# ReLU and row mean of a 67 MB array on one core: a second block of one row to a partition, and 126 rows a partition in place of 127

## The chip, the cores and the metric

One core of a Trainium2 chip. The metric is the device time of one execution in microseconds (us).

## The reference

```python
x = np.random.randn(32, 512, 1024).astype(np.float32)   # 16,384 rows of 4 KiB
np.mean(np.maximum(x, 0), axis=-1)                       # 16,384 results
```

## The kernel before

The first 128 rows are loaded one to a partition (a "block"). They come first and give ScalarE (ACT) early work; its table load of 1.28 us falls there. The other 16,256 rows are cut into 128 runs of J = 127, one run for each partition, so that rows of neighbouring partitions lie 127 x 4 KiB = 508 KiB apart in HBM. They come as seven full tiles of 16 rows a partition through three buffers, then pieces of 7, 4, 2 and 1 rows, then the last row in three pieces of columns. SyncE issues every transfer; the trace books each in packets, here one for each partition. ACT takes the even rows, VectorE (DVE) the odd ones; each writes one sum a row.

```python
xfirst, xmain = xf[:P, :], xf[P:, :]
outfirst, outmain = out.flatten()[:P], out.flatten()[P:]
J = J - 1                                     # 127
xr = xmain.rearrange("(p j) d -> p j d", p=P, j=J)
...
row_pieces = [7, 4, 2, 1]
col_pieces = [512, 256, 256]
...
for t in range(full):                         # 7 tiles, BUFS = 3, NB = 16
    buf_free(t)                               # waits for the tile 3 back to be consumed
    if t == 0:
        load(-1, row0[:, :], xfirst)          # the block: 128 packets of 4 KiB
    load(t, bufs[t % BUFS][:, :, :], xr[:, t * NB:(t + 1) * NB, :])   # 128 packets of 64 KiB
    if t == BUFS:
        nc.sync.wait_ge(first, 2)
        nc.sync.dma_start(                    # the block's results: 4 rows of 32 numbers
            out=outfirst.rearrange("(q i) -> q i", i=32), in_=turned0[0:P:32, :],
        ).then_inc(stored, 16)
... # pieces of rows, then of columns
nc.sync.dma_start(out=outr, in_=res[:, :]).then_inc(stored, 16)       # 128 rows of 508 B
...
nc.sync.wait_ge(stored, 32).then_inc(stored, -32)                     # the program's last wait
```

The block's 128 means lie one to a partition; DVE transposes them so that they leave as 4 rows of 128 B.

Of the kernel before, what the change touches and what calls it, by code (L numbers as in the profile page):

```python
# [9 lines left out]
ACT = mybir.ActivationFunctionType  # L10
# [35 lines left out]
def kernel(  # L46
# [10 lines left out]
    nc = tc.nc  # L57
    P = nc.NUM_PARTITIONS
    xf = x.flatten_outer_dims()
    R, D = xf.shape  # L60
    assert R % P == 0
    J = R // P
    inv = 1.0 / D

    xfirst, xmain = xf[:P, :], xf[P:, :]
    outfirst, outmain = out.flatten()[:P], out.flatten()[P:]
    J = J - 1
    xr = xmain.rearrange("(p j) d -> p j d", p=P, j=J)
    outr = outmain.rearrange("(p j) -> p j", p=P, j=J)

    NB = 16
    BUFS = 3
    full = J // NB

    row_pieces = [7, 4, 2, 1]
    assert full * NB + sum(row_pieces) + 1 == J
    col_pieces = [512, 256, 256]
    assert sum(col_pieces) == D

    def sbuf(name, *shape):  # L80
        return ctx.enter_context(nc.sbuf_tensor(name, list(shape), F32))

    bufs = [sbuf(f"rows{b}", P, NB, D) for b in range(BUFS)]
    sums, res, part = sbuf("sums", P, J), sbuf("res", P, J), sbuf("part", P, 2)


    last = sbuf("last", P, D + 2)
    scale = sbuf("scale", P, D // 4 + 2)

    row0, mean0, turned0 = sbuf("row0", P, D), sbuf("mean0", P, 32), sbuf("turned0", P, 32)  # L90


    loaded = [nc.alloc_semaphore(f"loaded{i}") for i in range(full + len(row_pieces) + len(col_pieces) + 1)]
    act, dve, pool = (nc.alloc_semaphore(n) for n in ("act", "dve", "pool"))
    first = nc.alloc_semaphore("first")
    stored = nc.alloc_semaphore("stored")
# [11 lines left out]
    def load(i, dst, src):  # L108
        nc.sync.dma_start(out=dst, in_=src).then_inc(loaded[i], 16)

    def buf_free(t):

        if t >= BUFS:
            nc.sync.wait_ge(act, t - BUFS + 1)
            nc.sync.wait_ge(dve, t - BUFS + 1)

    for t in range(full):
        buf_free(t)
        if t == 0:
            load(-1, row0[:, :], xfirst)  # L120
        load(t, bufs[t % BUFS][:, :, :], xr[:, t * NB:(t + 1) * NB, :])
        if t == BUFS:

            nc.sync.wait_ge(first, 2)
            nc.sync.dma_start(
                out=outfirst.rearrange("(q i) -> q i", i=32), in_=turned0[0:P:32, :],
            ).then_inc(stored, 16)
    j0 = full * NB
    buf_free(full)
    xt = bufs[full % BUFS]  # L130
    lo, i = 0, full
    for n in row_pieces:
        load(i, xt[:, lo:lo + n, :], xr[:, j0 + lo:j0 + lo + n, :])
        lo, i = lo + n, i + 1
    c = 0
    for w in col_pieces:
        load(i, last[:, c:c + w], xr[:, J - 1, c:c + w])
        c, i = c + w, i + 1
# [5 lines left out]
    def rows(i, xt, lo, n, j0):  # L144
        nc.scalar.wait_ge(loaded[i], 16)
        nc.vector.wait_ge(loaded[i], 16)
        for k in range(lo, lo + n):
            j = j0 + k
            done = (dve_row if j % 2 else act_row)(nc, xt[:, k, :], sums[:, j:j + 1])
            if k >= lo + n - 2:  # L150
                done.then_inc(dve if j % 2 else act, 1)

    def finish(after, lo, hi):

        nc.gpsimd.wait_ge(act, after)
        nc.gpsimd.wait_ge(dve, after)
        nc.gpsimd.tensor_scalar(  # L157
            out=res[:, lo:hi], in0=sums[:, lo:hi], scalar1=inv, scalar2=0.0, op0=ALU.mult, op1=ALU.add,
        )

    nc.scalar.wait_ge(pool, 1)
    nc.vector.wait_ge(pool, 1)
    nc.scalar.wait_ge(loaded[-1], 16)
    nc.scalar.activation(  # L164
        out=row0[:, :], in_=row0[:, :], func=ACT.Relu, scale=inv, accum_out=mean0[:, 0:1],
    ).then_inc(first, 1)
    nc.vector.wait_ge(first, 1)
    nc.vector.transpose(turned0[:, :], mean0[:, :]).then_inc(first, 1)  # L168
    for t in range(full):
        rows(t, bufs[t % BUFS], 0, NB, t * NB)  # L170
    finish(full, 0, j0)
    lo, i = 0, full
    for n in row_pieces[:-1]:
        rows(i, xt, lo, n, j0)
        lo, i = lo + n, i + 1
# [12 lines left out]
        out=res[:, J - 2:J - 1], in0=part[:, 0:1], scalar1=part[:, 1:2], scalar2=inv, op0=ALU.add, op1=ALU.mult,  # L188
# [9 lines left out]
        out=last[:, 768:], in0=last[:, 768:], scalar=0.0, in1=scale[:, :], op0=ALU.max, op1=ALU.mult,  # L198
        accum_out=res[:, J - 1:J],
# [7 lines left out]
    used = [s.num for s in (*loaded, act, dve, pool, first)]  # L207
    assert used == list(range(used[0], used[0] + len(used)))
    nc.sync.sem_clear(range(used[0], used[-1] + 1))
    nc.sync.wait_ge(stored, 32).then_inc(stored, -32)  # L210

    for e, hint in zip(hinted, hints):
        e.br_lt(flag, 1, on_true="rows_begin", on_false="rows_end").branch_hint(hint)
# [34 lines left out]
```

## Time and profile before

| what | value | from |
|---|---|---|
| device time, median of 3 | 161.46 us (161.40 to 161.55) | the runs |
| span of the profiled execution | 160.2 us | page |
| transfer engines busy | 97.7% | page, queue line |
| DVE / ACT busy | 46% / 44% | page |
| one full tile of 8.39 MB | 19.34 to 19.50 us | its landing times in the timeline |
| last packet of the loads ended | 157.38 us | records of single packets |
| last byte of the final store / its completion | 159.76 / 160.21 us | the same |

The page and the timeline lines that carry the reading are in the prediction.

```profile
SPq L115 <- DVE rows L20: 104.6, 5, 29.5
SPq L204 <- DVE last L197: 45.6, 1, 45.6
SPq L210 <- SPq L210: 1.2, 1, 1.2
```

The first line is SyncE waiting for buffers to come free, far ahead of need; the second is the wait for the last arithmetic; the third is the wait for the final store to be confirmed, and nothing runs beside it. It is 1.2 us of pure path.

### The profile page before, as it was taken

Reading aid. Unit: us, or ns where it says so; the run is one execution under the profiler, and the core shown is the slowest. Engines: PE = TensorE matmul, PEld = TensorE weight load, DVE = VectorE, ACT = ScalarE, POOL = GpSimd, SP = SyncE. Lnnn points to the kernel's source line nnn. Section 1 sums busy time; section 2 is a strip of 40 time slices with the busy share of each in tenths; the row PEclk is TensorE's granted clock in tenths of the full one; section 3 lists DMA queues with packets and bytes.
Section 4 is the critical chain, followed back from the end, with each engine's and each line's share of the span. In section 5 each row is a group of like instructions: output and inputs, shape, how many; then the busy total and the mean of one; then the engine's idle time right before and its main releaser. Section 6 shows DMA issues by size and latency. Waiting matters only on the chain. (4 is left out here: it accounts for less than half of the span.)

```text
span 160.2 us, 347 instructions
## 1 busy us (share of the span) xinstructions
DVE 73.3 (46%) x131; ACT 70.4 (44%) x133; POOL 1.3 (1%) x9
## 2 busy tenths in 40 slices
DVE  0000029900498006960079500993009920299984
ACT  1400029800496006950079300991009900299983
POOL 1000000000000000000000000000000000000001
DMA  9969969979989899699699699699699797998992
GB/s 393 507 278 523 507 278 523 442 344 523 409 376 523 360 425 524 294 491 523 262 524 523 262 523 524 262 523 523 262 524 458 327 523 327 425 451 367 419 412 102
DMA packets 2312, 67.18 MB, mean 419 GB/s; under 512 B 392, under 2 KB 648, under 8 KB 1032
## 3 DMA queue, kind: packets, MB, share of 16 engines
q1 hardware_dynamic: 2312, 67.18, 97.7%
HBM read 67.11 MB, written 0.07 MB: 419 GB/s over the span
## 5 line engine op out<-in xcount | busy, mean ns | idle before, releaser
L20 DVE TENSOR_SCALAR_CACHE_REDUCE rows<-rows 128x1024 f32<-128x1024 f32 (+1 forms) x63 | 72.1, 1208 | 78.9 <-DMA rows<-in_x_dram 78.7
L15 ACT ACTIVATE rows<-rows 128x1024 f32<-128x1024 f32 x64 | 66.2, 1035 | 84.1 <-DMA rows<-in_x_dram 83.9
L15 ACT ACTIVATION_READ_ACCUMULATOR rows<-rows 128x1 f32 x64 | 11.9, 186 | 0.0
L20 DVE DVE_READ_ACCUMULATOR rows<-rows 128x1 f32 x63 | 5.2, 82 | 0.0
L168 DVE STREAM_TRANSPOSE turned<-mean 128x32 f32<-128x32 f32 x1 | 0.2, 213 | 5.9 <-ACT row L164 5.9
L164 ACT ACT_TABLE_LOAD x1 | 1.3, 1283 | 3.3 <-DMA row<-in_x_dram 3.3
L157 POOL TENSOR_SCALAR res<-sums 128x112 f32<-128x112 f32 (+1 forms) x2 | 0.5, 250 | 154.0 <-DVE rows L20 154.0
L164 ACT ACTIVATE row<-row 128x1024 f32<-128x1024 f32 x1 | 1.1, 1056 | 0.0
L15 ACT ACTIVATE last<-last 128x512 f32<-128x512 f32 x1 | 0.6, 630 | 0.0
L20 DVE TENSOR_SCALAR_CACHE_REDUCE last<-last 128x256 f32<-128x256 f32 x1 | 0.4, 420 | 0.3 <-DMA last<-in_x_dram 0.3
L197 DVE SCALAR_TENSOR_TENSOR last<-last,scale 128x258 f32<-128x258 f32 x1 | 0.4, 428 | 0.1
L142 POOL MEMSET scale<- 128x258 f32 x1 | 0.3, 314 | 0.0
L187 POOL TENSOR_SCALAR res<-part 128x1 f32<-128x1 f32 x1 | 0.3, 267 | 0.6 <-DVE rows L20 0.6
L164 ACT ACTIVATION_READ_ACCUMULATOR row<-row 128x1 f32 x1 | 0.2, 186 | 0.0
L15 ACT ACTIVATION_READ_ACCUMULATOR last<-last 128x1 f32 x1 | 0.2, 186 | 0.0
L141 POOL MEMSET mean<- 128x32 f32 x1 | 0.1, 126 | 1.5 <-POOLq L55 1.5
L232 POOL MEMSET const-uint8-127<- 128x1 uint8 x1 | 0.1, 103 | 0.0
L232 POOL MEMSET const-bfloat16-1.0<- 128x1 bf16 x1 | 0.1, 102 | 0.0
L232 POOL MEMSET const-float32-0.0<- 128x1 f32 x1 | 0.1, 99 | 0.2 <-issue 0.2
L232 POOL MEMSET const-float32-1.0<- 128x1 f32 x1 | 0.1, 99 | 0.0
L20 DVE DVE_READ_ACCUMULATOR last<-last 128x1 f32 x1 | 0.1, 83 | 0.0
L197 DVE DVE_READ_ACCUMULATOR last<-last,scale 128x1 f32 x1 | 0.1, 82 | 0.0
## 6 DMA issues: line engine op xcount, KB each, us to landing
rows<-in_x_dram SPq DMA_DIRECT2D x1, 3584.0 KB, 38.1
rows<-in_x_dram SPq DMA_DIRECT2D x1, 2048.0 KB, 42.6
rows<-in_x_dram SPq DMA_DIRECT2D x1, 1024.0 KB, 44.7
row<-in_x_dram SPq DMA_DIRECT2D x1, 512.0 KB, 3.3
rows<-in_x_dram SPq DMA_DIRECT2D x1, 512.0 KB, 45.4
last<-in_x_dram SPq DMA_DIRECT2D x1, 256.0 KB, 45.6
last<-in_x_dram SPq DMA_DIRECT2D x2, 128.0 KB, 45.4
rows<-in_x_dram SPq DMA_DIRECT2D x7, 48.8
```

Of the source, the lines that this page charges most:

```text
L15: return nc.scalar.activation(out=src, in_=src, func=ACT.Relu, accum_out=acc)
L20: return nc.vector.tensor_scalar(out=src, in0=src, scalar1=0.0, scalar2=init, op0=ALU.max, op1=ALU.add, accum_out=acc,)
L141: nc.gpsimd.memset(mean0[:, :], 0.0)
L142: nc.gpsimd.memset(scale[:, :], inv).then_inc(pool, 1)
L157: nc.gpsimd.tensor_scalar(out=res[:, lo:hi], in0=sums[:, lo:hi], scalar1=inv, scalar2=0.0, op0=ALU.mult, op1=ALU.add,)
L164: nc.scalar.activation(out=row0[:, :], in_=row0[:, :], func=ACT.Relu, scale=inv, accum_out=mean0[:, 0:1],).then_inc(first, 1)
L168: nc.vector.transpose(turned0[:, :], mean0[:, :]).then_inc(first, 1)
L187: nc.gpsimd.tensor_scalar(out=res[:, J - 2:J - 1], in0=part[:, 0:1], scalar1=part[:, 1:2], scalar2=inv, op0=ALU.add, op1=ALU.mult,).then_i ...
L197: nc.vector.scalar_tensor_tensor(out=last[:, 768:], in0=last[:, 768:], scalar=0.0, in1=scale[:, :], op0=ALU.max, op1=ALU.mult, accum_out=r ...
L232: nc = _bacc.Bacc("TRN2", target_bir_lowering=False, num_devices=1)
```

## The change

A second block of 128 rows is taken out of the main part. J falls from 127 to 126, the distance between partitions from 508 to 504 KiB, the first short piece from 7 to 6 rows. The second block is loaded ahead of tile 2, behind the second full tile. Both blocks' means leave later, in two stores. The total of bytes is the same. What might be hoped for is one row less to compute a partition behind the last full tile, and a different pitch in HBM.

```diff
-    xfirst, xmain = xf[:P, :], xf[P:, :]
-    outfirst, outmain = out.flatten()[:P], out.flatten()[P:]
-    J = J - 1
+    xfirst, xmain = xf[:2 * P, :].rearrange("(c p) d -> p c d", c=2), xf[2 * P:, :]
+    outfirst, outmain = out.flatten()[:2 * P], out.flatten()[2 * P:]
+    J = J - 2
...
-    row_pieces = [7, 4, 2, 1]
+    row_pieces = [6, 4, 2, 1]
...
-        if t == 0:
-            load(-1, row0[:, :], xfirst)
+        if t in (0, 2):
+            c = t // 2
+            load(c - 2, row0[:, c, :], xfirst[:, c, :])
         load(t, bufs[t % BUFS][:, :, :], xr[:, t * NB:(t + 1) * NB, :])
-        if t == BUFS:
+        if t == BUFS + 2:
 
             nc.sync.wait_ge(first, 2)
-            nc.sync.dma_start(
-                out=outfirst.rearrange("(q i) -> q i", i=32), in_=turned0[0:P:32, :],
-            ).then_inc(stored, 16)
+            for c in range(2):
+                nc.sync.dma_start(
+                    out=outfirst[c * P:(c + 1) * P].rearrange("(q i) -> q i", i=32), in_=turned0[c:P:32, :],
+                ).then_inc(stored, 16)
... (ACT takes block c ahead of tile 0 and tile 2; DVE transposes behind the second)
-    nc.sync.wait_ge(stored, 32).then_inc(stored, -32)
+    nc.sync.wait_ge(stored, 48).then_inc(stored, -48)
```

More of the change, by code (lines that the diff above doesn't have):

```diff
@@ L88 @@
     scale = sbuf("scale", P, D // 4 + 2)
-    row0, mean0, turned0 = sbuf("row0", P, D), sbuf("mean0", P, 32), sbuf("turned0", P, 32)
-    loaded = [nc.alloc_semaphore(f"loaded{i}") for i in range(full + len(row_pieces) + len(col_pieces) + 1)]
+    row0, mean0, turned0 = sbuf("row0", P, 2, D), sbuf("mean0", P, 32), sbuf("turned0", P, 32)
+    loaded = [nc.alloc_semaphore(f"loaded{i}") for i in range(full + len(row_pieces) + len(col_pieces) + 2)]
     act, dve, pool = (nc.alloc_semaphore(n) for n in ("act", "dve", "pool"))
@@ L162 @@
     nc.vector.wait_ge(pool, 1)
-    nc.scalar.wait_ge(loaded[-1], 16)
-    nc.scalar.activation(
-        out=row0[:, :], in_=row0[:, :], func=ACT.Relu, scale=inv, accum_out=mean0[:, 0:1],
-    ).then_inc(first, 1)
-    nc.vector.wait_ge(first, 1)
-    nc.vector.transpose(turned0[:, :], mean0[:, :]).then_inc(first, 1)
-    for t in range(full):
+    for t in range(full):
+        if t in (0, 2):
+            c = t // 2
+            nc.scalar.wait_ge(loaded[c - 2], 16)
+            done = nc.scalar.activation(
+                out=row0[:, c, :], in_=row0[:, c, :], func=ACT.Relu, scale=inv, accum_out=mean0[:, c:c + 1],
+            )
+            if c == 1:
+                done.then_inc(first, 1)
+                nc.vector.wait_ge(first, 1)
+                nc.vector.transpose(turned0[:, :], mean0[:, :]).then_inc(first, 1)
         rows(t, bufs[t % BUFS], 0, NB, t * NB)
```

## The prediction

> **What bounds the kernel now.** I read the page first: the strip of 40 slices, the queue line, and the two costliest groups.
>
> ```profile
> DMA  9969969979989899699699699699699797998992
> q1 hardware_dynamic: 2312, 67.18, 97.7%
> HBM read 67.11 MB, written 0.07 MB: 419 GB/s over the span
> ...
> L20 DVE TENSOR_SCALAR_CACHE_REDUCE rows<-rows 128x1024 f32<-128x1024 f32 (+1 forms) x63 | 72.1, 1208 | 78.9 <-DMA rows<-in_x_dram 78.7
> L15 ACT ACTIVATE rows<-rows 128x1024 f32<-128x1024 f32 x64 | 66.2, 1035 | 84.1 <-DMA rows<-in_x_dram 83.9
> ```
>
> The packets of the one queue fill 97.7% of the 16 transfer engines' span. VectorE (DVE) and ScalarE (ACT) are each idle longer (78.9 and 84.1 us) than they are busy, nearly all of it waiting for the input. The dips to 6 in the strip are no gaps: a packet is booked where it starts and lasts 2.4 us of a 4 us slice. So next I asked for busy time by stage, taking as edges the moments at which the full tiles landed (when DVE and ACT start on them together).
>
> ```profile
> core 0: us, DVE busy (x) ACT busy (x) POOL busy (x), PEclk, DMA share, GB/s
> 42.32:61.69 19.37, 9.21 (x16) 8.42 (x16) 0.00 (x0) 1.00 1.00 433
> 61.69:81.05 19.36, 9.21 (x16) 8.43 (x17) 0.00 (x0) 1.00 1.00 433
> 81.05:100.40 19.35, 9.21 (x16) 8.42 (x16) 0.00 (x0) 1.00 1.00 434
> ```
>
> Every 8.39 MB tile takes 19.35 to 19.37 us with the transfer share at 1.00, and leaves DVE 10.1 us of slack. The kernel is a stream of 67.11 MB at 433 GB/s with a short start and a short tail. The tail I read from the timeline (start us, us, instruction, the idle time before it):
>
> ```profile
> 139.30 1.22 DVE L20 TENSOR_SCALAR_CACHE_REDUCE rows<-rows 128x1024 f32<-128x1024 f32 x1 [10.29 <-DMA rows<-in_x_dram]
> ...
> 152.71 1.22 DVE L20 TENSOR_SCALAR_CACHE_REDUCE rows<-rows 128x1024 f32<-128x1024 f32 x1 [0.79 <-DMA rows<-in_x_dram]
> ...
> 155.20 1.22 DVE L20 TENSOR_SCALAR_CACHE_REDUCE rows<-rows 128x1024 f32<-128x1024 f32 x1
> ...
> 156.49 0.75 DVE L20 TENSOR_SCALAR_CACHE_REDUCE rows<-rows 128x576 f32<-128x576 f32 x1
> ...
> 157.54 0.42 DVE L20 TENSOR_SCALAR_CACHE_REDUCE last<-last 128x256 f32<-128x256 f32 x1 [0.29 <-DMA last<-in_x_dram]
> ...
> 158.06 0.43 DVE L197 SCALAR_TENSOR_TENSOR last<-last,scale 128x258 f32<-128x258 f32 x1
> ...
> 158.57 0.35 SPq L205 DMA_DIRECT2D out_dram<-res  x1
> ```
>
> The last full tile is at hand at 139.30, the piece of four rows at 152.71, and the second column piece of the last row at 157.54. Each is still waited for, so the stream sets the tail too. From that last landing on, two short DVE instructions and the store follow in series.
>
> **What the Trainium skill says.** (1) "DMA: Bandwidth & Descriptors", section "Where 436 GB/s comes from", puts the ceiling of the 16 ports at 435.2 GB/s; the trace's 433 is 99.5% of it. (2) The same page, "Latency and other measured facts", in its entry on the HBM row pitch at large powers of two, has copies slow down at pitches of 512 KiB and beyond (207 GB/s at 512 KiB, 103 at 4 MiB) and recover with 4 KiB of padding. The pitch between partitions here is 127 rows of 4 KiB, 508 KiB, and becomes 504 KiB; the 433 GB/s agree that 508 is clean, and no trace yet shows 504. (3) The same page, "Why small descriptors are slow", states a fixed overhead for each packet; the trace has it, below. (4) The same page, "Why a DMA increments its semaphore by 16 and not by 1", derives how many engines share a transfer from the slowest dimension of its patterns: a store of 4 partitions uses 4 engines. The trace has just four packets of 128 B for it.
>
> **The change part by part.** The records of single packets in the trace give the median time of one packet by size, where all engines are busy: 65,536 B 2,420 ns; 28,672 B 1,062; 16,384 B 611; 4,096 B 159; 1,024 B 46. These lie on a line: (2,420 - 1,062)/36,864 = 0.0368 ns a byte, and 159 - 4,096 x 0.0368 = about 8.3 ns fixed. That is all I need to price the loads:
>
> - *Removed:* one of seven rows from the first short piece. Its 128 packets shrink from 28,672 to 24,576 B, 1,062 to about 913 ns. At 8 packets for each engine: 8 x 149 = 1.19 us less.
> - *Added:* a second block load of 128 packets of 4,096 B: 8 x 159 = 1.27 us for each engine, and one more completion write (9 ns). Bytes are unchanged; the sum is 8 x 8.3 ns + 9 ns = **about +0.08 us, and all of it on the path**, as the stream has no gap.
> - *Moved:* the block goes between tiles 1 and 2, so that tiles 2 to 6 land 1.27 us later and the pieces behind them only 0.08 us later. Three buffers are loaded ahead, and the issues of the later loads ran 27 us or more before their packets, so no transfer starts late.
> - *Compute:* one ACT row of 1.06 us + 0.19 us (its accumulator read) comes behind tile 1, into an idle stretch of 10.9 us; DVE's transpose (0.21 us) moves there and waits for it, inside its own 10.1 us. Neither reaches tile 2, expected near 61.69 + 1.27 = 62.96. The table load of 1.28 us still hides behind the first block. In the first short piece DVE keeps 3 rows and ACT goes from 4 to 3.
> - *Store:* two stores of 512 B in place of one, later. Each takes about 0.63 us of the issuing queue with two tiles of packets still ahead, and four packets of 13 ns. Nothing. The final store has 504 B a row instead of 508 (27 ns a packet): nothing.
> - *Tail:* tile 6 lands later (139.30 + 1.27 + a little = 140.6), while what follows it does not. DVE needs 1.14 us a row: 8 rows until 149.7, 3 rows of the short piece until 153.1. The piece of four landed at 152.8, so here DVE is 0.3 us late where it had been 0.79 us early. Two rows: 155.4, against 155.3 of the piece of two; one row: 156.55, against 156.57 for the next landing. The lateness is gone by then, and another 0.29 us lie before the column piece. ACT, at 1.04 us a row, finishes the short piece near 152.2 and is never late. So the tail moves by the stream's 0.08 us alone.
>
> Sum: 161.46 + 0.08 = 161.54; with a few hundredths for a crowded tail, **161.55 us**.
>
> **The rivals.** *The pitch matters.* Multiples of 8 KiB instead of 4 KiB could make the streams of the 16 engines meet in the same part of HBM more often. For it speaks point (2), where powers of two are costly; against it that 504 KiB is 63 x 8 KiB, far from a large power of two, and that the present stream is held by the ports and not by HBM, which leaves HBM some reserve. If each 64 KiB packet took 3% longer, 2,420 to 2,493 ns, the 56 of them for each engine would add 4.1 us: 165.6 us. Half of that would still be called the same.
> *The pitch helps.* It can't by much: from 433.3 to 435.2 GB/s is 0.4% of 154.9 us, 0.7 us: 160.8 us at the least.
> *DVE becomes the end of the tail.* The margin above is 0.02 us at the piece of one row and 0.29 us behind it. If the later tile costs DVE 0.5 us more than I worked out, the end moves by perhaps 0.2 us: 161.75 us. Speaks for it that DVE has no idle time left between 140.6 and 157.4; against it that its rows took 1.14 us without a change all through the trace.
> *The block's load is slow in mid-stream.* The first packets of the first block took up to 656 ns (the trace's records), but those started on idle engines; the 4,096 B packets of the one-row piece, in the stream, took 159. If all eight took 300 ns, it would add 1.1 us: 162.7 us. I give it little.
>
> **Range and chances.** The three runs of before spread 0.15 us. Around 161.55 I allow 0.35 us below for another draw of the stream's rate and 0.55 us above for the tail and a slightly worse pitch: 161.2 to 162.1. Faster by 2% would be below 158.2, under the floor of the ports: 0.01. Slower by 2% is above 164.7; only the pitch could do that: 0.05. Within 2%: 0.94.
>
> **What would show it.** Right: tile 2 waited for until about 63.0 instead of 61.69, the intervals of the later tiles again 19.35 to 19.4 us, 24,576 B packets near 913 ns, 4,096 B ones at 159; in the tail no wait of DVE before the pieces of four and two rows, but still one before the column piece, at about 157.6. Wrong: 64 KiB packets clearly off 2,420 ns, in either direction (the pitch); DVE's last wait gone (the tail); a longer stretch between tiles 1 and 2 than 19.37 + 1.3 us (the block); a transfer share under 1.00 in any stage between full tiles (a late issue).

## The result, and the profile after

The changed kernel took 161.72 us (median of 6 runs, 161.50 to 162.07) against 161.43 us of the kernel before in the same rounds (161.26 to 161.78). The ratio is 1.0016, with a 95% interval of 1.0000 to 1.0032: the same. A ratio is the mean time of one kernel's fast runs over that of the other's of the same rounds, so it is not quite the ratio of the medians.

The page of the changed kernel, the same lines:

```profile
DMA  9969969979996996996996996996998998899991
q1 hardware_dynamic: 2464, 67.18, 97.5%
HBM read 67.11 MB, written 0.07 MB: 419 GB/s over the span
...
L20 DVE TENSOR_SCALAR_CACHE_REDUCE rows<-rows 128x1024 f32<-128x1024 f32 (+1 forms) x63 | 71.9, 1208 | 84.7 <-DMA rows<-in_x_dram 84.7
```

There are 2,464 packets instead of 2,312, the same bytes, and the queue is as full as before. DVE's idle time grew only because its early wait for the block's transpose is now a wait for tile 0. By stage, from landing to landing of the full tiles (us, busy times, clock, transfer share, GB/s):

```profile
42.44:63.06 20.62, 9.42 (x17) 9.46 (x18) 0.00 (x0) 1.00 1.08 465
63.06:82.42 19.36, 9.21 (x17) 8.43 (x17) 0.00 (x0) 1.00 1.00 433
82.42:101.76 19.34, 9.21 (x16) 8.42 (x17) 0.00 (x0) 1.00 1.00 434
101.76:121.11 19.35, 9.20 (x16) 8.42 (x16) 0.00 (x0) 1.00 1.00 434
```

The first row holds tile 2 and the block: 20.62 us where the same stage had 19.37, so the block took 1.25 us of the stream. (Its share over 1 is the booking of packets where they start.) The stages behind it are the old 19.35 us. The tail, from the timeline:

```profile
140.46 1.22 DVE L20 TENSOR_SCALAR_CACHE_REDUCE rows<-rows 128x1024 f32<-128x1024 f32 x1 [10.14 <-DMA rows<-in_x_dram]
...
153.00 1.21 DVE L20 TENSOR_SCALAR_CACHE_REDUCE rows<-rows 128x1024 f32<-128x1024 f32 x1
...
155.28 1.22 DVE L20 TENSOR_SCALAR_CACHE_REDUCE rows<-rows 128x1024 f32<-128x1024 f32 x1
...
156.45 0.75 DVE L20 TENSOR_SCALAR_CACHE_REDUCE rows<-rows 128x576 f32<-128x576 f32 x1
...
157.48 0.42 DVE L20 TENSOR_SCALAR_CACHE_REDUCE last<-last 128x256 f32<-128x256 f32 x1 [0.27 <-DMA last<-in_x_dram]
...
158.00 0.43 DVE L203 SCALAR_TENSOR_TENSOR last<-last,scale 128x258 f32<-128x258 f32 x1
...
158.51 0.35 SPq L211 DMA_DIRECT2D out_dram<-res  x1
```

The last tile came 1.16 us later (140.46 against 139.30), DVE no longer waited before the piece of four rows (153.00), and the lateness was gone before the column piece, for which it again waited 0.27 us. The final store was issued at 158.51, even 0.06 us earlier than before. Yet the span is 160.5 us, not 160.2. The rest is in SyncE's own waits (waited for: us in total, times, longest):

```profile
SPq L210 <- DVE last L203: 40.8, 1, 40.8
SPq L216 <- SPq L216: 1.5, 1, 1.5
```

The last line is the wait for the final store, 1.5 us against 1.2. In the packet records the last byte of that store was moved at 159.70 us and its last completion arrived at 160.43, 0.73 us later; before, these were 159.76 and 160.21, 0.44 us. So of the 0.22 us between the two spans, -0.06 lie ahead of the store's last byte and +0.28 behind it (0.726 less 0.444). I had priced the stores at nothing.

The -0.06 does not mean that the packets cost nothing. In the profile of the kernel before, the last two stages were slower than the 19.35 us of the others:

```profile
100.40:119.80 19.40, 9.20 (x16) 8.42 (x16) 0.00 (x0) 1.00 1.00 432
119.80:139.30 19.50, 9.21 (x16) 8.42 (x17) 0.00 (x0) 1.00 0.93 400
```

Counted in packets: the time by which 65,536 B packets exceeded 2,418 ns, added up and divided by the 16 engines, is 0.67 us there and 0.42 us in the changed kernel's profile, 0.25 us less. With the 0.08 us of added packets the loads should then have ended about 0.17 us earlier, and they did (157.21 against 157.38 us). A single pair of profiles can't show the packet price without this correction.

### The profile page after: what moved, and what is told of

Same layout as the page of the kernel before. It is cut to its first block, busy times and chain, and to the rows that moved or that the text cites. A ratio compares the mean times of both kernels' runs of the same rounds, so it can differ in the third digit from the quotient of the medians.

```text
span 160.5 us, 349 instructions
## 1 busy us (share of the span) xinstructions
DVE 73.1 (46%) x131; ACT 70.3 (44%) x133; POOL 1.3 (1%) x9
## 2 busy tenths in 40 slices
DMA packets 2464, 67.18 MB, mean 419 GB/s; under 512 B 416, under 2 KB 672, under 8 KB 1184
## 3 DMA queue, kind: packets, MB, share of 16 engines
q1 hardware_dynamic: 2464, 67.18, 97.5%
## 5 line engine op out<-in xcount | busy, mean ns | idle before, releaser
L15 ACT ACTIVATE rows<-rows 128x1024 f32<-128x1024 f32 (+1 forms) x63 | 65.2, 1035 | 84.2 <-DMA rows<-in_x_dram 84.0
L169 ACT ACTIVATE row<-row 128x1024 f32<-128x1024 f32 x2 | 2.1, 1048 | 0.0
```

The source lines that it names most:

```text
L15: return nc.scalar.activation(out=src, in_=src, func=ACT.Relu, accum_out=acc)
L169: done = nc.scalar.activation(out=row0[:, c, :], in_=row0[:, c, :], func=ACT.Relu, scale=inv, accum_out=mean0[:, c:c + 1],)
```

## The experiments

Two theories were on the table for a difference this small. **A**: only the packets cost (+0.08 us), the rest is spread. **B**: the final store's confirmation is really slower. The doubts that the prediction had left, pitch and block, were tested beside them. All times are medians; "before" is the kernel before in the same rounds.

### again: the changed kernel unaltered

> The changed kernel, unaltered, in five rounds. Theory A (only the packets cost): the ratio to the kernel before is 1.0005 (+0.08 us), and the +0.26 us of the first rounds was run-to-run spread. Theory B (the final store is slower with rows of 504 B than of 508 B: in the two profiles the last loads were done within 0.17 us of each other, and the wait behind the store lasted 1.5 us against 1.2): the ratio stays near 1.0016 (+0.26 us), and the wait behind the store is again 1.4 to 1.5 us. An interval that holds both leaves it open.

Measured: 161.62 us against 161.57 (ratio 1.0004, interval 0.9988 to 1.0021). The interval holds 0.08 us and 0.26 us alike. The wait behind the store was again long:

```profile
SPq L216 <- SPq L216: 1.4, 1, 1.4
```

Pooling this with the first rounds, the changed kernel's 12 runs average 161.74 us and the 17 of the kernel before 161.54: 0.20 us, an eighth of a per cent. By the spread of these runs that is uncertain by about 0.17 us either way (two standard errors), so 0.08 us is not excluded.

### pitch508 and pitch512: the distance between partitions alone

```diff
-    xr = xmain.rearrange("(p j) d -> p j d", p=P, j=J)
+    xr = xf[P:, :].rearrange("(p j) d -> p j d", p=P, j=J + 1)[:, :J, :]    # pitch508
+    xr = xf.rearrange("(p j) d -> p j d", p=P, j=J + 2)[:, :J, :]           # pitch512
```

> The changed kernel with one thing undone: the rows of the full tiles and pieces are read 127 rows apart from partition to partition (508 KiB) instead of 126 (504 KiB), so the result is wrong on purpose, and packets, sizes and order are the same. If the pitch of 504 KiB costs nothing (my prediction), this takes the changed kernel's time within 0.15 us, and the 65,536 B packets stay at 2,418 to 2,420 ns. If 504 KiB costs the 0.2 us that the first rounds showed beyond the packets, this is 0.2 us faster.

> The same with partitions 128 rows apart (512 KiB), wrong on purpose. The Trainium skill's entry on row pitches gives 207 GB/s at 512 KiB against 214 at full rate for copies. If that holds for one-way loads too, the 65,536 B packets take 3% longer (2,490 ns) and the time is near 166 us. If the load stream is held by the ports and HBM has reserve, nothing changes: 161.7 us, and then a pitch of 504 KiB can't matter either.

Measured, both with the wrong result they were meant to have: 161.71 us at 508 KiB (ratio 1.0006, 0.9990 to 1.0023) and 161.81 us at 512 KiB (1.0013, 0.9992 to 1.0034), before 161.57. The changed kernel in the same rounds had 161.62. The 65,536 B packets had a median of 2,418 ns in all three. The stages between full tiles of the kernel with 512 KiB:

```profile
63.32:82.67 19.35, 9.21 (x17) 8.43 (x17) 0.00 (x0) 1.00 1.00 434
82.67:102.04 19.37, 9.21 (x17) 8.43 (x17) 0.00 (x0) 1.00 1.01 433
102.04:121.49 19.45, 9.20 (x16) 8.42 (x16) 0.00 (x0) 1.00 1.00 431
```

The stream runs at 431 to 434 GB/s even at the distance that I thought the risky one. A 3% loss, 4 us, is excluded; a few tenths of a microsecond are not, by the interval. The pitch is no lever for this kernel.

### store508, store508_again: the changed kernel with the old stores

```diff
-            for c in range(2):
+            for c in range(1):
...
-    outr = outmain.rearrange("(p j) -> p j", p=P, j=J)
+    outr = outmain.rearrange("(p j) -> p j", p=P, j=J + 1)     # res has a filler column
...
-    nc.sync.wait_ge(stored, 48).then_inc(stored, -48)
+    nc.sync.wait_ge(stored, 32).then_inc(stored, -32)
```

> The changed kernel with the stores of the kernel before: one store of 512 B and a final store of 128 rows of 508 B (the last column is filler, the result is wrong on purpose), loads and arithmetic as in the changed kernel. Theory A: the changed kernel's time, within 0.1 us. Theory B: 0.2 us faster than the changed kernel, and the wait behind the final store back at 1.2 us from 1.5.

> The same program as in the run with the old stores, which came out 0.29% slower than the kernel before where theory B wanted it level and theory A 0.05% slower. If that was an effect of the program, it repeats: about 1.003. If it was chance, this lands between 0.999 and 1.0015.

Measured: 161.98 us (ratio to before 1.0029, 1.0010 to 1.0049), and in another set of rounds 161.99 us (1.0026, 1.0013 to 1.0038). Neither theory had that: putting the old stores back did not make it faster but, if anything, slower than the changed kernel (by the means 0.28 us in the same rounds, 162.03 against 161.74), and the distance to the kernel before repeats. Why it is slower than the changed kernel stays open. The wait behind the store:

```profile
SPq L217 <- SPq L217: 1.5, 1, 1.5
```

It stayed long with rows of 508 B. So theory B as I had put it, that rows of 504 B alone are the cause, falls.

### control: the kernel before against itself

> The kernel before against itself, to learn how far two identical programs come apart. If the interval that the rounds give is honest, the ratio lies within 0.1% of 1. If a difference of 0.2 to 0.3 us shows here too, then neither the +0.26 us of the first rounds of the change nor the +0.4 us of the run with the old stores can be read as an effect. Its profile is a second look at the wait behind the final store: 1.2 us again if that is a property of the kernel, 1.2 to 1.7 if it is spread.

Measured: 161.59 us against 161.47, ratio 1.0000, interval 0.9987 to 1.0013. Identical programs agree to about 0.13%, 0.2 us. This is the grain of every figure here. The wait behind its final store:

```profile
SPq L210 <- SPq L210: 1.3, 1, 1.3
```

### before_store504: the kernel before with the new stores alone

```diff
-    outr = outmain.rearrange("(p j) -> p j", p=P, j=J)
+    outr = outmain.rearrange("(p j) -> p j", p=P, j=J - 1)
... (two early stores of 512 B as in the change, the final one of res[:, :J - 1])
```

> The kernel before with the stores of the changed one alone: two stores of 512 B and a final store of 504 B a row (one result column and some rows go amiss, wrong on purpose); loads and arithmetic as before. Theory A: 1.000, within 0.1%. Theory B (these stores cost 0.2 us): 1.0015 and a wait behind the final store of 1.4 us or more.

Measured: 161.79 us against 161.47, ratio 1.0022, interval 1.0008 to 1.0036, with the old loads untouched. The wait:

```profile
SPq L211 <- SPq L211: 1.5, 1, 1.5
```

The interval leaves out theory A's 1.000, though not quite the tenth of a per cent that I had allowed it; the wait is the one that theory B asked for. Together with store508, the long wait comes with the new stores on old loads and with the old stores on new loads.

### rowloads: the packet term magnified

```diff
-        load(t, bufs[t % BUFS][:, :, :], xr[:, t * NB:(t + 1) * NB, :])
+        if t < BUFS:
+            load(t, bufs[t % BUFS][:, :, :], xr[:, t * NB:(t + 1) * NB, :])
+        else:
+            for k in range(NB):
+                load(t, bufs[t % BUFS][:, k, :], xr[:, t * NB + k, :])
... (ACT and DVE wait for all 16 transfers of such a tile)
```

> The changed kernel with tiles 3 to 6 loaded as 16 transfers of one row to a partition each: the same bytes in packets of 4,096 B, 128 such packets an engine for each tile in place of eight of 65,536 B. It magnifies the term that I put on the path. My model: 8.3 ns for each of (128 - 8) x 4 = 480 more packets an engine, 4.0 us, and 60 more completion writes of 9 ns, 0.5 us: 166.1 us, ratio to before 1.028, each of those tiles 20.5 us instead of 19.36. If small packets overlap better than that in the stream, so that their fixed time does not reach the end, the time stays at 161.7 us, and the added block was free.

Measured: 166.82 us against 161.47, ratio 1.0324 (1.0308 to 1.0339). The stages of tiles 3 to 6:

```profile
63.12:83.59 20.47, 9.21 (x17) 8.43 (x17) 0.00 (x0) 1.00 1.03 412
83.59:104.07 20.48, 9.20 (x17) 8.42 (x17) 0.00 (x0) 1.00 1.03 410
104.07:124.53 20.46, 9.20 (x16) 8.42 (x16) 0.00 (x0) 1.00 1.03 409
124.53:145.45 20.92, 9.21 (x16) 8.42 (x16) 0.00 (x0) 1.00 1.05 422
```

Three stages show the 20.5 us that the model gave, the fourth 0.4 us more. Together they are 82.33 us; the same four of the changed kernel ran from 63.06 to 140.46, 77.40. That is 4.93 us for the 4.5 expected. DVE and ACT were as busy as ever and much less than the stage: the packets' fixed time goes straight to the end. The term is real and about a tenth larger than I had it (the median 4,096 B packet took 161 ns here, 159 elsewhere). The total, 166.82 us, is 0.7 us above the 166.1 expected, the fourth stage's 0.4 us among it. Scaled down, 4.93 us for 480 packets an engine is about 10 ns a packet, completion writes included; for the eight added packets of the change's block that is again about 0.08 us, an estimate, since no pair of runs is fine enough to show it.

### placebo and laterstore: is it any alteration, or the place of the early store?

```diff
+    nc.gpsimd.memset(part[:, :], 0.0)          # placebo: one more short instruction at the start
```
```diff
-        if t == BUFS:                          # laterstore: the early store moves behind tile 5
+        if t == BUFS + 2:
```

> The kernel before with one more short memset of GpSimd at the start, on a tile that is written again later: loads, stores and the tail are untouched. It asks whether any change of the program moves the wait behind the final store. In the two profiles of the kernel before the last completion came 0.44 and 0.49 us after the last byte of that store; in the seven of altered kernels 0.65 to 0.96 us. If that follows from the change's loads or stores, this stays at 0.45 to 0.5 us and at a ratio of 1.000. If any altered program shows it, this has 0.65 us or more and a ratio of 1.001 to 1.002.

> The kernel before with its one early store of 512 B issued behind the load of tile 5 instead of tile 3, as the change does; nothing else. If the place of the early store delays the completion of the final one: 0.65 us or more from its last byte to its completion, and a ratio of 1.0015. If not: 0.45 to 0.5 us and 1.000.

Measured, before 161.65 us: placebo 161.43 (ratio 0.9986, 0.9973 to 1.0000), laterstore 161.68 (1.0007, 0.9985 to 1.0028). The wait behind the store, placebo and then laterstore:

```profile
SPq L211 <- SPq L211: 1.2, 1, 1.2
```
```profile
SPq L210 <- SPq L210: 1.2, 1, 1.2
```

From the last byte to the last completion it was 0.47 and 0.41 us. Neither "any other program" nor "the early store comes later" explains the long wait.

### store512: rows of 512 B, no early store

```diff
-    outr = outmain.rearrange("(p j) -> p j", p=P, j=J)
+    outr = out.flatten().rearrange("(p j) -> p j", p=P, j=J + 1)   # and the early store is taken out
```

> The kernel before with no early store and a final store of 128 rows of 512 B that begin at multiples of 512 B (a filler column, wrong on purpose). If the late completions come from rows that begin and end inside a memory line[...], all 16 engines finish together here, 0.25 to 0.3 us after the last byte, and the time is about 0.2 us under the kernel before: ratio 0.999. If it is not the rows, the last completion again comes 0.45 us or more after the last byte and the ratio is 1.000.

Measured: 161.29 us against 161.65, ratio 0.9989, interval 0.9973 to 1.0005, result wrong as intended. The last completion came 0.35 us after the last byte, between the two outcomes I had named, though the 16 completions did come together (0.18 to 0.35 us). It is the shortest seen, but the interval holds 1 and the early store was removed with it: inconclusive on the rows. That memory has lines in which the place of a row matters was a guess, and no run shows it.

### front: both blocks at the start

```diff
-        if t in (0, 2):
-            c = t // 2
+        for c in range(2 if t == 0 else 0):
             load(c - 2, row0[:, c, :], xfirst[:, c, :])
...
-    issue_ahead_of_entry_barrier(nc, 2)       # that many loads are issued ahead of the entry barrier
+    issue_ahead_of_entry_barrier(nc, 3)
```

> The changed kernel with the second block loaded straight behind the first, ahead of tile 0, instead of behind tile 1. Same packets, same bytes, other order. If only packets count, its time is the changed kernel's, 161.7 us within 0.15; tile 0 is at hand at 24.3 us instead of 23.1. If the block disturbs the stream where it stood, or if two small loads at the start leave the engines unfed, it differs by more.

Measured: 162.53 us against 161.65, ratio 1.0051 (1.0031 to 1.0072). The mean of its runs, 162.43 us, is 0.78 us above that of the kernel before in the same rounds (161.65), where the changed kernel was 0.20 us above: about 0.6 us more than the changed kernel, and I had expected at most 0.15: a miss. Tile 0 was at hand at 24.16 us as expected, and tile 2 at 62.94 us, where the changed kernel had 63.06. The loss came later:

```profile
82.36:101.74 19.38, 9.21 (x16) 8.42 (x16) 0.00 (x0) 1.00 1.00 433
101.74:121.46 19.72, 9.20 (x16) 8.42 (x16) 0.00 (x0) 1.00 1.00 425
121.46:140.98 19.52, 9.21 (x17) 8.43 (x17) 0.00 (x0) 1.00 0.92 396
```

The last two stages took 0.4 and 0.2 us more than 19.35. The excess of the 65,536 B packets over 2,418 ns, per engine as above, is 1.01 us here, 0.42 in the first profile of the changed kernel and 0.67 before. But it was 1.14 us in the profile of the same changed kernel's second look, at 162.25 us the slowest of that kernel's runs. So that excess varies with the execution by as much as the kernels differ. Five of front's six runs were above 162.2 us, but only one of them has packet records; whether all were slow for this reason, and why front should be slow more often, is open. Nothing points to the start being a better place for the block, and no run pointed to a version clearly better than the kernel before.

### What is left open

The wait behind the final store, in all fourteen profiles:

| kernel | wait, us | last byte to last completion, us | transfers in the program |
|---|---|---|---|
| before, control, placebo, laterstore | 1.2, 1.3, 1.2, 1.2 | 0.44, 0.49, 0.47, 0.41 | 17 |
| store512 | 1.1 | 0.35 | 16 |
| before_store504 | 1.5 | 0.73 | 18 |
| store508, store508_again | 1.5, 1.6 | 0.75, 0.84 | 18 |
| the change, again, front, pitch508, pitch512 | 1.5, 1.4, 1.4, 1.4, 1.7 | 0.73, 0.65, 0.65, 0.66, 0.96 | 19 |
| rowloads | 1.6 | 0.80 | 79 |

The two groups do not overlap, so run-to-run spread is an unlikely cause. Nor is it the chip: the record names the chip of all runs but the first pair, three chips in all, and both groups occur on two of them. In each of the slow ones a part of the 16 completions comes 0.17 to 0.45 us behind the rest; in before_store504 it is just two. The device times point the same way. The means of the seven sets of runs with 18 or 19 transfers, front left aside, lie 0.11 to 0.45 us above the kernel before in their rounds (all but before_store504 hold the 0.08 us of packets as well); those of control, placebo, laterstore and store512 lie between 0.22 us below and 0.09 above. Placebo's 0.22, with the same loads and stores as before, tells how much noise is in such means. It is not the row size alone, not the place of the early store, not the mere fact of another program. What does divide the table is the number of transfers, 17 or fewer against 18 or more, and with it the number of packets, at most 2,312 against at least 2,320; but that is read from the table after the fact, and no run varied the count alone. One more tiny transfer in the kernel before would test it. The cause stays open.

## Why the prediction was right or wrong

- **The bound** was right. The stages behind the block took 19.34 to 19.36 us each, 433 to 434 GB/s where the window shows it, and neither DVE nor ACT took a place on the path between tiles. The prediction's "Every 8.39 MB tile takes 19.35 to 19.37 us" was read from three of six stages; the others took 19.34, 19.40 and 19.50 us, a variation larger than the effect that it priced.
- **The packet prices** were right. The 24,576 B packets took 912 ns (median) for about 913 estimated, the 4,096 B ones 159. Rowloads, which magnifies this term, shows that it does reach the end, at 4.93 us for 4.5.
- **The move** was right: tile 2 at 63.06 us for 62.96, and the added stage time 1.25 us for 1.27.
- **The tail** was right in its order and nearly in its times: 153.00 (153.1), 155.28 (155.4), 156.45 (156.55), 157.48 (157.6), and the wait before the column piece 0.27 us for 0.29. The rival of DVE becoming the end did not happen.
- **The pitch** was right to be left out, and more safely than I knew: 512 KiB does no harm that these rounds could show either. That the ports hold the stream and HBM has reserve was argued for it; the runs agree, but none tests that reason.
- **The block in mid-stream**, the last rival, did not come: 1.25 us is the price of ordinary packets.
- **The stores** were wrong. Of the final one the prediction says "(27 ns a packet): nothing". The packets were indeed the same, but I had priced only the moving of bytes and not the confirmation behind them, which nothing overlaps. It grew by 0.28 us between the two profiles; before_store504 shows that the new stores bring a long wait even with the old loads, and store508 that the new loads do so even with the old stores.

The sum thus left out a term, and was probably too small: 0.08 us where 0.20 us, give or take 0.17, is the best figure (12 and 17 runs pooled). The range of 161.2 to 162.1 held 161.72 because it had been given room for the tail and the pitch, neither of which used it; that this room also covered the store was luck. The share of the store in that 0.20 us can't be measured finer than the grain of 0.2 us that the control shows.

## What to carry to other kernels

When one stream of transfers sets the time, price a change by its packets in that stream, fixed time and bytes, and treat the work beside it as free until the timeline of the tail says otherwise. Then look at what nothing overlaps: the wait for the last store is pure path, and a change that seems to leave that store alone can come with a longer one. Run the kernel against itself before reading anything into a tenth of a per cent.

## What the Trainium skill lacked or had wrong

- "DMA: Bandwidth & Descriptors", section "Latency and other measured facts", the entry on the HBM row pitch: it tells of copies, 207 GB/s at 512 KiB. It does not say that a plain load in 64 KiB packets is spared: at 512 KiB this one kept 431 to 434 GB/s and a median of 2,418 ns a packet.
- The same page, section "Why small descriptors are slow", gives the fixed overhead of a packet as about 3 cycles and not in ns (a note to the same page's table of transfers issued from GpSimd has about 10.5 ns a packet for its smallest one). For loads in packets of 1 to 64 KiB these traces fit 8.3 ns, and rowloads, which pays it 480 times more for each engine, came out about a tenth above that.
- The same page, section "Anatomy of one DMA — SWDGE (gpsimd) path", puts most of a transfer's fixed time down to the write receipt, for transfers issued from GpSimd. No page says that the confirmation of nearly the same small store, here issued from SyncE, can differ between programs: 0.35 to 0.49 us from last byte to last completion in five profiles, 0.65 to 0.96 in nine.
